# Seven-product pairs: product F in another PSUM bank, and sums, casts and low parts in another order

## The chip, the core and the metric

The kernel runs on one core of a Trainium2 chip. The metric is the time of one execution in microseconds on the device, as the median of timed runs. The engines are TensorE (PE in the profile; PEld is its weight load), VectorE (DVE), ScalarE (ACT), GpSimd (POOL) and SyncE (SP, which issues most transfers). Each works through its own queue in order, and engines wait for each other by semaphores.

## The reference

The reference is a two-layer block over 512 latent tokens of width 1024. What matters here is the MLP that ends each layer, and of it the one of the second layer:

```
def _sq_relu_mlp(h, w1, w2):
    return jnp.square(jax.nn.relu(h @ w1)) @ w2
...
h_lat = h_lat + mod_l[5] * _sq_relu_mlp(
    _modulate(_rmsnorm(h_lat, norm2_g[i]), mod_l[3], mod_l[4]), mlp_w1[i], mlp_w2[i])
```

`w1` is 1024 x 4096 and `w2` 4096 x 1024. All is float32 in and out.

## The kernel before

**High and low parts.** TensorE multiplies in `fp32r`. To keep precision, each operand is split: ScalarE casts it to a high part (line 163), and VectorE or POOL subtracts that from the source for the low part (line 164). A product is then three sets of matmuls: weights' high by activations' high, weights' high by activations' low, weights' low by activations' high.

**Blocks.** `mlp` runs four blocks of 1024 hidden columns. In a block a first phase makes the hidden tiles (f = 0 to 7: square of relu of `h @ w1`, as `gh` and `gl`), and a second phase multiplies them by `w2` (output tiles called `r`, eight weights). In the second layer, blocks 1 to 3 make their hidden tiles two at a time with `pair7`: four pairs in a block, 12 in all. Block 0 makes the activation sums that this needs (`act_sums`, the tiles `th`, split partly by POOL).

**A pair.** Two hidden tiles (2 x 128 columns) by 512 tokens are a 2 x 2 problem of blocks, and `pair7` forms it from seven products instead of eight. Each product is 12 matmuls of 128x256 (lines 1655, 1656, 1658). They are called A to G here, in the order in which TensorE has them:

| Product | Written to | Weights | 
|---|---|---|
| A, B | `px[:, x]`, `py[:, x]` | two halves of `w0` |
| C | `py[:, y]` | `w1`, first half |
| D | `pz[:, y]` | `w2`, first half |
| E | `px[:, y]` | `w3` |
| F | `px[:, x]` again | `w1`, second half |
| G | `pz[:, x]` | `w2`, second half |

`px`, `py` and `pz` are PSUM tiles of one bank each; `x` and `y` are their halves of 256 columns. A wait is set for a whole tile: TensorE may not write one half while an earlier reader of the other half has not finished.

VectorE joins the products: the sum `s1` of `py` and the copy `p1` of A (line 1715); `u3` from E (1721); two more sums into `s1` from D and F (1722, 1725); `s2` from G (1729). The `finish` function that a pair returns is called in the next pair: three ScalarE instructions for each of the two hidden tiles (relu, square to `gh`, square in place), and VectorE's low part `gl` for each (1741).

**Weights.** Of the four weights of a pair, `w0` is the raw weight k. `w1` is made from two sums by VectorE (`pair_sums`, lines 1430 and 1431), `w2` is the raw weight k + 1 after POOL has added its own halves (1439, the "second sum" here), and `w3` is a sum of two raw halves by POOL (1438, "early sum" here). VectorE makes the low parts of `w1` and `w2`, POOL those of `w0` and `w3`. `w_fetch` issues the transfers of raw weights on SP, `w_prep` makes the next weights ready. The order of each engine's queue is the order in which this code is written.

Of the kernel before, what the change touches and what calls it, by code (L numbers as in the profile page):

```python
# [12 lines left out]
ALU = mybir.AluOpType  # L13
# [8 lines left out]
T = 512  # L22
# [71 lines left out]
def body(ctx: ExitStack, tc: tile.TileContext, I, out):  # L94
    nc = tc.nc
    act = nc.scalar
    dve = nc.vector
    pool = nc.gpsimd
    pe = nc.tensor

    def f32(ap):
        return ap.bitcast(F32)
# [46 lines left out]
    def nm(s):  # L149
        cnt[0] += 1  # L150
        return f"{s}_{cnt[0]}"
# [10 lines left out]
    def split(hi, lo, src, lo_eng=None):  # L162
        act.copy(out=hi, in_=src)  # L163
        (lo_eng or dve).tensor_tensor(out=lo, in0=src, in1=f32(hi), op=ALU.subtract)  # L164
# [5 lines left out]
    def wfetch(src, which="s"):  # L170
        pl, tg, nr, nb, rp = streams[which]
        raw = rp.tile([P, 1024], F32, name=nm("raw"), tag=tg + "raw", bufs=nr)
        nc.sync.dma_start(out=raw, in_=src)
        return raw

    def wload(src, lo_eng, which="s", raw=None):
        pl, tg, nr, nb, rp = streams[which]
        if raw is None:
            raw = wfetch(src, which)
        hi = pl.tile([P, 1024], F32R, name=nm("whi"), tag=tg + "whi", bufs=nb)  # L180
        lo = pl.tile([P, 1024], F32R, name=nm("wlo"), tag=tg + "wlo", bufs=nb)
        split(hi, lo, raw, lo_eng)
        return hi, lo
# [22 lines left out]
    def proj(*a, late=0):  # L206
        for _ in proj_steps(*a, late=late):
            pass
# [93 lines left out]
    w3 = st.tile([P, 1024], F32, name="w3", tag="swhi", bufs=2)  # L302
# [56 lines left out]
    def row_load(k):  # L359
# [11 lines left out]
        out=sil, in0=e16.rearrange("p (s k) -> p s k", s=2), in1=prm[:, 0:16].rearrange("p (s k) -> p s k", s=2), op=ALU.mult  # L371
# [1004 lines left out]
    for d in range(3):  # L1376
        for k in (6, 7):
            out_part(8 * d + k)
        dve.scalar_tensor_tensor(
            out=hs[d], in0=r_pre[d], scalar=g1[:, d : d + 1], in1=hs[d], op0=ALU.mult, op1=ALU.add  # L1380
# [10 lines left out]
    def ps_m(name):  # L1391
        return ps.tile([P, T], F32, name=nm(name), tag="mm", bufs=6)
# [10 lines left out]
    wraw, wsp = [], []  # L1403
    fast = set(range(9)) | set(range(65, 77)) - {73}

    def w_fetch(n):
        while len(wraw) < min(n, len(wsrc)):
            k = len(wraw)
            wraw.append(ahead.pop(3 + k) if k < 3 else wfetch(wsrc[k], "st"[k % 2]))
# [2 lines left out]

    pairs, sums_done, scr = set(), set(), [None]

    def w_split(k, src, eng, n=1024):
        pl, tg, nr, nb, rp = streams["st"[k % 2]]
        hi = pl.tile([P, 1024], F32R, name=nm("whi"), tag=tg + "whi", bufs=nb)
        lo = pl.tile([P, 1024], F32R, name=nm("wlo"), tag=tg + "wlo", bufs=nb)  # L1420
        split(hi[:, :n], lo[:, :n], src, eng)
        return hi, lo

    def pair_sums(k):

        if k in sums_done or k not in pairs:
            return
        sums_done.add(k)
        a, b, t = wraw[k], wraw[k + 1], scr[0]
        dve.tensor_tensor(out=t[:, :T], in0=b[:, :T], in1=a[:, :T], op=ALU.add)  # L1430
        dve.tensor_tensor(out=t[:, T : 2 * T], in0=t[:, :T], in1=a[:, T:], op=ALU.add)

    def w_prep(n):
        while len(wsp) < min(n, len(wsrc)):
            k = len(wsp)
            if k in pairs:
                a, b, t = wraw[k], wraw[k + 1], scr[0]
                pool.tensor_tensor(out=t[:, 2 * T : 3 * T], in0=a[:, :T], in1=b[:, :T], op=ALU.add)
                pool.tensor_tensor(out=b[:, :T], in0=b[:, :T], in1=b[:, T:], op=ALU.add)
                wsp.append(w_split(k, a, pool))  # L1440
            elif k - 1 in pairs:
                pair_sums(k - 1)
                wsp.append(w_split(k, scr[0][:, : 2 * T], dve))
            else:
                eng = (dve, pool)[k // 2 % 2]
                wsp.append(wload(None, pool if k in fast else eng, "st"[k % 2], wraw[k]))
# [3 lines left out]
    def w_next(lead=2):  # L1450

        k = wk[0]
        wk[0] += 1
        w_fetch(k + 7)
        w_prep(k + 1 + lead)
        return wsp[k]
# [162 lines left out]
    def mlp(layer, ah_, al_, nrm, i_norm, shift_in, last_norm, mod_next, load=None, seven=True):  # L1619
# [25 lines left out]
        def b_part(half, t):  # L1645
            seg = slice(t * 256, (t + 1) * 256)
            return [(ah_[half * 4 + i][:, seg], al_[half * 4 + i][:, seg]) for i in range(4)]

        def t_part(n):
            return [(th[:, i, 0, n, :], th[:, i, 1, n, :]) for i in range(4)]  # L1650

        def product(o, w, c, b):
            for i in range(4):
                l = w[0][:, c + i * P : c + (i + 1) * P]
                pe.matmul(o, l, b[i][0], start=(i == 0), stop=False)  # L1655
                pe.matmul(o, l, b[i][1], start=False, stop=False)  # L1656
            for i in range(4):
                pe.matmul(o, w[1][:, c + i * P : c + (i + 1) * P], b[i][0], start=False, stop=(i == 3))  # L1658
        for blk in range(4):
# [35 lines left out]
            def pair7(f, before):  # L1695

                k = wk[0]
                wk[0] += 2
                w_fetch(k + 7)
                w0, w1 = wsp[k], wsp[k + 1]  # L1700
                w2 = w_split(k, wraw[k + 1], dve)
                x, y = slice(0, 256), slice(256, 512)
                px, py, pz = ps_m("f"), ps_m("f"), ps_m("f")
                small = [ml.tile([P, 256], F32, name=nm("na"), tag="na", bufs=4) for _ in range(2)]
                p1, u3 = small
                s1 = ml.tile([P, T], F32, name=nm("r"), tag="r", bufs=3)
                twice = lambda v: v.rearrange("p (a t) -> p a t", a=1).to_broadcast([P, 2, 256])
                both = lambda v: v.rearrange("p (a t) -> p a t", a=2)
                product(px[:, x], w0, 0, b_part(0, 0))
                act.copy(out=p1, in_=px[:, x])  # L1710
                product(py[:, x], w0, T, b_part(1, 0))
                w3 = w_split(k + 1, scr[0][:, 2 * T : 3 * T], pool, T)
                before(0)
                product(py[:, y], w1, 0, t_part(2))
                dve.tensor_tensor(out=both(s1), in0=both(py), in1=twice(p1), op=ALU.add)
                before(1)
                w_fetch(k + 9)
                w_prep(k + 3)
                product(pz[:, y], w2, 0, t_part(0))
                product(px[:, y], w3, 0, t_part(1))  # L1720
                dve.tensor_tensor(out=u3, in0=px[:, y], in1=s1[:, y], op=ALU.add)  # L1721
                dve.tensor_tensor(out=s1[:, y], in0=pz[:, y], in1=s1[:, y], op=ALU.add)
                pair_sums(k + 2)
                product(px[:, x], w1, T, b_part(1, 1))
                dve.tensor_tensor(out=s1[:, y], in0=px[:, x], in1=s1[:, y], op=ALU.add)
                w_prep(k + 4)
                product(pz[:, x], w2, T, [(ah_[i][:, y], al_[i][:, y]) for i in range(4)])
                s2 = ml.tile([P, T], F32, name=nm("r"), tag="r", bufs=3)
                dve.tensor_tensor(out=both(s2), in0=both(pz), in1=twice(u3), op=ALU.add)
                for u in range(2):  # L1730
                    mk = att_tile if f + u < 4 else w_tile
                    gh[f + u], gl[f + u] = mk("gh"), mk("gl")

                def finish(part):
                    for u, s, sign in ((0, s1, 1.0), (1, s2, -1.0)):
                        if part != 1:
                            act.activation(out=s, in_=s, func=AF.Relu, scale=sign)
                            act.activation(out=gh[f + u], in_=s, func=AF.Square)
                            act.activation(out=s, in_=s, func=AF.Square)
                        if part != 0:  # L1740
                            dve.tensor_tensor(out=gl[f + u], in0=s, in1=f32(gh[f + u]), op=ALU.subtract)

                return finish

            f0 = 0
            if blk == 0:
                f0 = 4
                n = 256
# [31 lines left out]
            if blk and seven:  # L1780
                fin7 = lambda part: None
                for f in range(0, 8, 2):
                    fin7 = pair7(f, fin7)
                fin7(2)
            else:
                for f in range(f0, 8):
                    w = w_next()
                    pp = f_tile(f)
                    proj(pp, w, ah_, al_)
                    f_out(f, 0, T, pp)  # L1790
                    if blk:
                        grow()
# [108 lines left out]
    for hf, (t0, n) in enumerate(SEG):  # L1901
        for d in range(ND):
# [4 lines left out]
            for k in range(3):  # L1907
                t = hf + k
                a, b = zh[t][d // 4][:, cs_], zl[t][d // 4][:, cs_]
# [225 lines left out]
```

## Time and profile before

| | us |
|---|---|
| Median of three runs | 1133.67 (1132.42 to 1134.82) |
| Profiled execution, its own time | 1134.61 |
| Its span (first to last instruction) | 1132.8 |
| PE busy | 1083.6 (96% of the span) |
| DVE busy | 769.3 (68%) |
| POOL busy | 492.3 (43%) |
| ACT busy | 480.3 (42%) |

The three blocks of pairs lie at about 844 to 897, 940 to 986 and 1030 to 1076 us of the span. The busy shares are means over the whole program; what an instruction waits for is read from the stretch in which it stands. A row's last bracket gives how long the engine had been idle before it and whose end it waited for.

### The profile page before, as it was taken

How to read it: one execution, taken by the hardware profiler on the slowest of the kernel's cores; microseconds unless marked ns; L12 is line 12 of the kernel's file. 1: busy time of each engine (PE TensorE's matmuls, PEld its weight loads, DVE VectorE, ACT ScalarE, POOL GpSimd, SP SyncE). 2: the span in 40 equal slices, each digit the busy share in tenths (PEclk: the TensorE clock that was granted, in tenths of full speed). 3: DMA queues.
4: the chain of work that ended last, by engine and by line, in shares of the span. 5: the costliest groups of instructions: out<-in, count | busy, mean ns of one | idle time of the engine just before them, and what ended most of it. 6: DMA issues, size and time to landing. Idle time of an engine off the chain costs nothing.

```text
span 1132.8 us, 15916 instructions
## 1 busy us (share of the span) xinstructions
PE 1083.6 (96%) x6172; PEld 934.0 (82%) x6172; DVE 769.3 (68%) x1114; ACT 480.3 (42%) x812; POOL 492.3 (43%) x364
## 2 busy tenths in 40 slices
PE   8899999999999999999999999899998899999896
PEld 5488988888989988888888888899878888889886
DVE  6589899989856746676686684776457626725844
ACT  4454246666544531341241232565325614713531
POOL 4457237785654322122122133363576525443512
PEclk9899999999999999999999999999999999999998
DMA  9776754125432336557567553122312322332212
GB/s 336 271 268 207 248 171 144 67 69 171 157 124 75 113 111 242 170 196 248 169 204 252 173 189 128 38 68 83 110 62 89 114 75 75 112 112 75 75 38 75
DMA packets 48654, 161.42 MB, mean 142 GB/s; under 512 B 5250, under 2 KB 8578, under 8 KB 48452
## 3 DMA queue, kind: packets, MB, share of 16 engines
q1 hardware_dynamic: 46132, 149.93, 38.6%
q0 software_dynamic: 2448, 10.49, 2.6%
q8 instruction: 48, 0.79, 0.3%
q14 instruction: 26, 0.21, 0.1%
HBM read 156.20 MB, written 4.20 MB: 142 GB/s over the span
## 4 chain that ended last, share of the span: by engine, by line
PE 71%; DVE 14%; ACT 4%; issue 4%; DMA 3%; POOL 3%; SPq 0%; POOLq 0%; ACTq 0%; DVEq 0%
PE r L197 11%; PE r L199 10%; PE r L203 10%; PE f L199 6%; PE f L203 6%; PE f L197 6%; DVE g L629 3%; PE f L1655 2%; PE f L1658 2%; PE f L1656 2%; DMA g<-in_adaN 1%; DMA g<-in_adaT 1%; DVE nl L1542 1%; DVE scr L1430 1%; ACT whi L163 1%
## 5 line engine op out<-in xcount | busy, mean ns | idle before, releaser
L164 POOL TENSOR_TENSOR wlo<-raw,whi 128x1024 fp32r<-128x1024 f32 x77 | 191.5, 2489 | 360.0 <-ACT whi L163 305.4
L197 PE MATMUL r<-gh,whi 128*128 128x512 f32 (+1 forms) x576 | 207.3, 368 | 0.0
L199 PE MATMUL r<-gl,whi 128*128 128x512 f32 (+1 forms) x576 | 207.0, 368 | 0.0
L163 ACT CAST whi<-raw 128x1024 fp32r<-128x1024 f32 x135 | 139.3, 1042 | 126.4 <-PE r L199 102.1
L1555 DVE SCALAR_TENSOR_TENSOR h<-r,mods,h 128x512 f32<-128x512 f32 (+1 forms) x81 | 54.3, 671 | 149.4 <-PE r L203 149.2
L203 PE MATMUL r<-gh,wlo 128*128 128x512 f32 (+1 forms) x576 | 130.7, 368 | 0.0
L197 PEld LDWEIGHTS r<-gh,whi 128*128 128x128 f32 x576 | 108.3, 188 | 19.1
L199 PEld LDWEIGHTS r<-gl,whi 128*128 128x128 f32 x576 | 108.4, 188 | 18.9
L203 PEld LDWEIGHTS r<-gh,wlo 128*128 128x128 f32 x576 | 100.5, 188 | 18.9
L197 PE MATMUL f<-nh,whi 128*128 128x512 f32 (+1 forms) x320 | 116.0, 370 | 0.0
L199 PE MATMUL f<-nl,whi 128*128 128x512 f32 (+1 forms) x320 | 116.0, 370 | 0.0
L1484 DVE CUSTOM_DVE_ANT_0 g<-g,sbcl 128x1024 f32<-128x1024 f32 x48 | 105.1, 2191 | 0.0
L1673 DVE TENSOR_TENSOR r<-r 128x512 f32<-128x512 f32 (+1 forms) x48 | 37.6, 784 | 67.9 <-ACT gh L1672 67.8
L164 DVE TENSOR_TENSOR wlo<-raw,whi 128x1024 fp32r<-128x1024 f32 x58 | 75.0, 1294 | 12.2 <-ACT whi L163 12.2
L1671 ACT ACTIVATE r<-f 128x512 f32<-128x512 f32 (+1 forms) x48 | 25.1, 523 | 131.6 <-PE f L203 130.0
L203 PE MATMUL f<-nh,wlo 128*128 128x512 f32 (+1 forms) x320 | 73.1, 371 | 0.0
L199 PEld LDWEIGHTS f<-nl,whi 128*128 128x128 f32 x320 | 60.2, 188 | 10.8
L197 PEld LDWEIGHTS f<-nh,whi 128*128 128x128 f32 x320 | 60.2, 188 | 10.8
L203 PEld LDWEIGHTS f<-nh,wlo 128*128 128x128 f32 x320 | 56.3, 188 | 10.8
L197 PE MATMUL u<-ah,whi 128*128 128x512 f32 x160 | 63.4, 396 | 1.3 <-DVE v L884 1.3
L199 PE MATMUL u<-al,whi 128*128 128x512 f32 x160 | 62.5, 391 | 0.0
L1655 PE MATMUL f<-nh,whi 128*128 128x256 f32 x192 | 48.9, 287 | 13.9 <-DVE na L1721 13.9
(413 smaller groups left out, 2514.9 us busy)
## 6 DMA issues: line engine op xcount, KB each, us to landing
raw<-in_w SPq DMA_DIRECT2D x128, 512.0 KB, 4.5
g<-in_adaT SPq DMA_DIRECT2D x80, 512.0 KB, 4.0
g<-in_adaN SPq DMA_DIRECT2D x16, 512.0 KB, 9.1
raw<-in_w_hy SPq DMA_DIRECT2D x12, 512.0 KB, 4.3
raw<-in_w_qk SPq DMA_DIRECT2D x8, 512.0 KB, 4.0
pth<-in_pth POOLq DMA_DIRECT2D x4, 768.0 KB, 5.9
raw<-in_w_out SPq DMA_DIRECT2D x5, 512.0 KB, 3.6
x<-in_xT SPq DMA_DIRECT2D x8, 256.0 KB, 7.1
```

The lines of the kernel that those rows point to most:

```text
L163: act.copy(out=hi, in_=src)
L164: (lo_eng or dve).tensor_tensor(out=lo, in0=src, in1=f32(hi), op=ALU.subtract)
L197: pe.matmul(ps, wh[:, c], ah[i][:, t0 : t0 + n], start=(i == 0), stop=False)
L199: pe.matmul(ps, wh[:, c], al[i][:, t0 : t0 + n], start=False, stop=False)
L203: pe.matmul(ps, wl[:, i * P : (i + 1) * P], ah[i][:, t0 : t0 + n], start=False, stop=(i == k - 1))
L629: dve.tensor_tensor_reduce(out=g, in0=g, in1=sbc[0], scale=1.0, scalar=0.0, op0=ALU.mult, op1=ALU.add, accum_out=mods[:, 0, 2 + k // ND, k ...
L1484: dve.tensor_tensor_reduce(out=gin[k], in0=gin[k], in1=sbc[0], scale=1.0, scalar=0.0, op0=ALU.mult, op1=ALU.add, accum_out=mods[:, layer, ...
L1555: dve.scalar_tensor_tensor(out=hs[d][:, seg], in0=pp[:, :n], scalar=gate[:, d : d + 1], in1=hs[d][:, seg], op0=ALU.mult, op1=ALU.add)
L1655: pe.matmul(o, l, b[i][0], start=(i == 0), stop=False)
L1656: pe.matmul(o, l, b[i][1], start=False, stop=False)
L1671: act.activation(out=r, in_=pp[:, :n], func=AF.Relu)
L1673: dve.tensor_tensor(out=r, in0=r, in1=r, op=ALU.mult)
```

## The change

The change works in `pair7` and its helpers alone.

- F is written to `py[:, x]` instead of `px[:, x]`, and the sum behind it reads it there.
- POOL's two sums for the next pair get a function of their own, `pair_first`. It is called early in a pair, the first of the two sums ahead of the split of `w3`, the second behind it; for this the sum has two places in `scr` that take turns (`s3_part`).
- The split of `w3` (cast and low part) is moved from behind B to ahead of A.
- The weight sums of the next pair (`pair_sums`) are moved from behind VectorE's sums on D and E to ahead of them.
- `finish` now runs in four calls: ScalarE's three instructions of the first hidden tile, its low part, then (behind the cast of the next `w0`) ScalarE's three of the second, and its low part only after VectorE's sums on D and E.
- One fetch at the start of a pair, up to weight k + 7, takes the place of two, up to k + 6 and later k + 8.

```
-                w_fetch(k + 7)
+                w_fetch(k + 8)
+                pair_first(k + 2, 1)
                 w0, w1 = wsp[k], wsp[k + 1]
                 w2 = w_split(k, wraw[k + 1], dve)
+                w3 = w_split(k + 1, s3_part(k), pool, T)
+                pair_first(k + 2)
...
                 product(py[:, x], w0, T, b_part(1, 0))
-                w3 = w_split(k + 1, scr[0][:, 2 * T : 3 * T], pool, T)
                 before(0)
                 product(py[:, y], w1, 0, t_part(2))
                 dve.tensor_tensor(out=both(s1), in0=both(py), in1=twice(p1), op=ALU.add)
                 before(1)
-                w_fetch(k + 9)
                 w_prep(k + 3)
+                before(4)
+                pair_sums(k + 2)
                 product(pz[:, y], w2, 0, t_part(0))
                 product(px[:, y], w3, 0, t_part(1))
                 dve.tensor_tensor(out=u3, in0=px[:, y], in1=s1[:, y], op=ALU.add)
                 dve.tensor_tensor(out=s1[:, y], in0=pz[:, y], in1=s1[:, y], op=ALU.add)
-                pair_sums(k + 2)
-                product(px[:, x], w1, T, b_part(1, 1))
-                dve.tensor_tensor(out=s1[:, y], in0=px[:, x], in1=s1[:, y], op=ALU.add)
+                before(2)
+                product(py[:, x], w1, T, b_part(1, 1))
+                dve.tensor_tensor(out=s1[:, y], in0=py[:, x], in1=s1[:, y], op=ALU.add)
                 w_prep(k + 4)
...
-                        if part != 1:
+                        if part in (4 * u, 3):
...
-                        if part != 0:
+                        if part in (u + 1, 3):
```

```
+    def s3_part(k):
+        c = (2 + k // 2 % 2) * T
+        return scr[0][:, c : c + T]
+
+    def pair_first(k, n=2):
+
+        if k not in pairs:
+            return
+        a, b = wraw[k], wraw[k + 1]
+        if (k, 1) not in first_done:
+            first_done.add((k, 1))
+            pool.tensor_tensor(out=s3_part(k), in0=a[:, :T], in1=b[:, :T], op=ALU.add)
+        if n == 2 and (k, 2) not in first_done:
+            first_done.add((k, 2))
+            pool.tensor_tensor(out=b[:, :T], in0=b[:, :T], in1=b[:, T:], op=ALU.add)
```

Lines move by the added code: 1715, 1721, 1722, 1725, 1729 and 1741 become 1731, 1738, 1739, 1742, 1746 and 1758; 1438 and 1439 become 1444 and 1447.

VectorE's queue in the second pair of the first block, before. The tiles `f` are PSUM, `r` is `s1` or `s2`, `na` is `u3` or `p1`, `scr` and `raw` hold weights:

```order
L1715 TENSOR_TENSOR r_8092<-f_8088,na_8090 128x512
L1741 TENSOR_TENSOR gl_8080<-r_7967,gh_8079 128x512
L1741 TENSOR_TENSOR gl_8082<-r_8077,gh_8081 128x512
L1721 TENSOR_TENSOR na_8091<-f_8087,r_8092 128x256
L1722 TENSOR_TENSOR r_8092<-f_8089,r_8092 128x256
L1430 TENSOR_TENSOR scr_7169<-raw_7914,raw_7873 128x512
L1431 TENSOR_TENSOR scr_7169<-scr_7169,raw_7873 128x512
L1725 TENSOR_TENSOR r_8092<-f_8087,r_8092 128x256
```

The same place on VectorE after:

```order
L1731 TENSOR_TENSOR r_8100<-f_8096,na_8098 128x512
L1758 TENSOR_TENSOR gl_8078<-r_7975,gh_8077 128x512
L1430 TENSOR_TENSOR scr_7169<-raw_7914,raw_7873 128x512
L1431 TENSOR_TENSOR scr_7169<-scr_7169,raw_7873 128x512
L1738 TENSOR_TENSOR na_8099<-f_8095,r_8100 128x256
L1739 TENSOR_TENSOR r_8100<-f_8097,r_8100 128x256
L1758 TENSOR_TENSOR gl_8080<-r_8075,gh_8079 128x512
L1742 TENSOR_TENSOR r_8100<-f_8096,r_8100 128x256
```

The two weight sums stand ahead of `u3` and of the sum behind it now, one of the two low parts behind them; and the last row reads the tile of the first (`f_8096`, `py`) instead of that of `u3`.

POOL's queue from the same pair on, before (`wlo<-scr` is the low part of `w3`, `wlo<-raw` that of the next `w0`):

```order
L164 TENSOR_TENSOR wlo_8119<-scr_7169,whi_8118 128x512
L1438 TENSOR_TENSOR scr_7169<-raw_7873,raw_7914 128x512
L1439 TENSOR_TENSOR raw_7914<-raw_7914 128x512
L164 TENSOR_TENSOR wlo_8150<-raw_7873,whi_8149 128x1024
L164 TENSOR_TENSOR wlo_8252<-scr_7169,whi_8251 128x512
L1438 TENSOR_TENSOR scr_7169<-raw_7956,raw_8010 128x512
```

The same place on POOL after:

```order
L1444 TENSOR_TENSOR scr_7169<-raw_7873,raw_7914 128x512
L164 TENSOR_TENSOR wlo_8091<-scr_7169,whi_8090 128x512
L1447 TENSOR_TENSOR raw_7914<-raw_7914 128x512
L164 TENSOR_TENSOR wlo_8144<-raw_7873,whi_8143 128x1024
L1444 TENSOR_TENSOR scr_7169<-raw_7956,raw_7958 128x512
L164 TENSOR_TENSOR wlo_8224<-scr_7169,whi_8223 128x512
```

The early sum of the next pair stands ahead of the low part of `w3`, and so directly behind the 1024-wide low part of `w0` of the pair before.

## Rows read from the trace of the kernel before

**Rows 1.** Whom TensorE waited for: engine, line, releaser, us in total, times, longest.

```profile
PE f L1655 <- DVE na L1721: 13.9, 12, 1.6
```

**Rows 2.** Timeline of TensorE, first block: start us, length us, instruction, [idle before, releaser].

```profile
868.84 0.39 PE L1655 MATMUL f<-nh,whi 128*128 128x256 f32 x1 [1.59 <-DVE na L1721]
...
870.37 0.28 PE L1655 MATMUL f<-nh,whi 128*128 128x256 f32 x1
...
871.79 0.28 PE L1655 MATMUL f<-nh,whi 128*128 128x256 f32 x1
...
881.14 0.38 PE L1655 MATMUL f<-nh,whi 128*128 128x256 f32 x1 [1.59 <-DVE na L1721]
...
893.22 0.39 PE L1655 MATMUL f<-nh,whi 128*128 128x256 f32 x1 [1.37 <-DVE na L1721]
```

**Rows 3.** Timeline of VectorE, same stretch.

```profile
867.54 0.91 DVE L1741 TENSOR_TENSOR gl<-r,gh 128x512 fp32r<-128x512 f32 x1 [0.78 <-ACT r L1739]
868.37 0.41 DVE L1721 TENSOR_TENSOR na<-f,r 128x256 f32<-128x256 f32 x1
868.82 0.43 DVE L1722 TENSOR_TENSOR r<-f,r 128x256 f32<-128x256 f32 x1
869.62 2.86 DVE L1430 TENSOR_TENSOR scr<-raw,raw 128x512 f32<-128x512 f32 x1 [0.38 <-POOL raw L1439]
...
876.14 1.22 DVE L164 TENSOR_TENSOR wlo<-raw,whi 128x1024 fp32r<-128x1024 f32 x1
```

**Rows 4.** Timeline of POOL, same stretch.

```profile
869.55 2.38 POOL L164 TENSOR_TENSOR wlo<-raw,whi 128x1024 fp32r<-128x1024 f32 x1
```

**Rows 5.** Chain of waits, one turn of the ring: start us, length us, piece.

```profile
876.19 2.34 POOL wlo L164
...
880.28 1.62 POOL raw L1439
...
881.92 2.86 DVE scr L1430
...
884.81 0.70 DVE scr L1431
```

**Rows 6.** Timeline of ScalarE: first of six squares, and the cast behind them.

```profile
876.00 0.63 ACT L1737 ACTIVATE r<-r 128x512 f32<-128x512 f32 x1
...
879.71 1.03 ACT L163 CAST whi<-raw 128x1024 fp32r<-128x1024 f32 x1
```

**Rows 7.** Timeline of the second block: A, `p1`, `s1` of its first pair; F of its fourth.

```profile
940.37 0.28 PE L1655 MATMUL f<-nh,whi 128*128 128x256 f32 x1
...
941.98 0.38 ACT L1710 COPY na<-f 128x256 f32<-128x256 f32 x1 [2.68 <-PE f L1658]
...
944.87 0.69 DVE L1715 TENSOR_TENSOR r<-f,na 128x512 f32<-128x512 f32 x1 [2.42 <-PE f L1658]
...
983.12 0.39 PE L1655 MATMUL f<-nh,whi 128*128 128x256 f32 x1 [1.37 <-DVE na L1721]
```

**Rows 8.** Timeline of the first pair of the first block, several engines.

```profile
844.93 0.68 DVE L1430 TENSOR_TENSOR scr<-raw,raw 128x512 f32<-128x512 f32 x1
...
850.71 0.39 PE L1655 MATMUL f<-th,whi 128*128 128x256 f32 x1 [2.18 <-ACT th L163]
...
851.42 0.73 POOL L164 TENSOR_TENSOR nl<-b,nh 128x256 fp32r<-128x256 f32 x1
...
852.17 1.22 DVE L164 TENSOR_TENSOR wlo<-raw,whi 128x1024 fp32r<-128x1024 f32 x1 [1.55 <-ACT whi L163]
...
857.06 0.39 PE L1655 MATMUL f<-nh,whi 128*128 128x256 f32 x1 [0.52 <-DVE na L1721]
```

**Rows 9.** Stretches: us, busy (instructions) of PE, PEld, DVE, ACT, POOL; granted clock, DMA share, GB/s.

```profile
851.50:854.90 3.40, 3.39 (x17) 3.39 (x18) 1.83 (x2) 2.38 (x4) 2.46 (x3) 0.55 0.01 2
...
870.40:873.80 3.40, 3.40 (x31) 3.40 (x30) 3.10 (x3) 0.49 (x1) 1.53 (x1) 1.00 0.02 5
```

**Rows 10.** DMA issues on the page: transfer, queue, count, KB each, us to landing.

```profile
raw<-in_w SPq DMA_DIRECT2D x128, 512.0 KB, 4.5
```

More of the change, by code (lines that the diff above doesn't have):

```diff
@@ L1409, in w_fetch @@
             wraw.append(ahead.pop(3 + k) if k < 3 else wfetch(wsrc[k], "st"[k % 2]))
-    pairs, sums_done, scr = set(), set(), [None]
+    pairs, first_done, sums_done, scr = set(), set(), set(), [None]
     def w_split(k, src, eng, n=1024):
@@ L1436, in w_prep @@
             if k in pairs:
[L1437 to L1440, printed above, removed]
+                pair_first(k)
+                wsp.append(w_split(k, wraw[k], pool))
             elif k - 1 in pairs:
@@ L1783, in mlp @@
                     fin7 = pair7(f, fin7)
-                fin7(2)
+                fin7(3)
             else:
```

## Prediction

> **What bounds the kernel now.** I read first the page's busy shares (TensorE 96%), then whom TensorE waits for, then the stretch where it waits, engine by engine. The longest sum of waits is one group: the first matmul of product F waits for VectorE's `u3` (line 1721), 13.9 us in 12 times, once in each of the 12 pairs [rows 1]. Everything the change touches lies in these 12 pairs, so the rest of the 1132.8 us span is taken over as it is.
>
> In a pair without waits TensorE needs seven products. One is 1.42 us (871.79 less 870.37), so seven are 9.95 us; the pair from F to F lasts 12.30 us (881.14 less 868.84) [rows 2]. It is tempting to book the whole 1.59 us wait before F as a gain. But the rows of the other engines show why `u3` is late. VectorE reaches `u3` at 868.37, having waited for ScalarE before the second low part `gl` at 867.54 [rows 3]; and the chain of waits in this stretch runs not through TensorE but in a ring: POOL's low part (876.19) and second weight sum (880.28), VectorE's weight sums 1430 and 1431 (881.92, 884.81), then ScalarE's casts and squares, and round again [rows 5].
>
> The price inside this ring is that VectorE and POOL hold each other up. VectorE's sum 1430 lasts 2.86 us at 869.62 beside POOL's low part of 869.55 to 871.93, and ends 0.55 us after it [rows 3, 4]; with POOL idle the same sum is 0.68 us [rows 8]. The other way round, POOL's 512-wide low part (876.19, 2.34 us) ends 1.17 us after VectorE's low part of 876.14 to 877.36 [rows 3, 5]. VectorE's sums that read PSUM don't pay: `u3` takes 0.41 us at 868.37 while POOL works towards 869.55. So in these rows POOL's work and VectorE's work with two SBUF operands take turns, in the order in which they ask. The Trainium skill (SBUF — State Buffer, "Who interferes with whom") calls the shared pair an exclusive lock, held for a whole instruction; these rows agree, and the rule speaks against putting such a VectorE instruction between two that TensorE waits for. If POOL cost VectorE nothing, the stall below would be nil and the time that of the second rival.
>
> **The change, part by part.** Times in this part count from the first matmul of a pair's product A.
>
> *The banks.* F goes to `py[:, x]` instead of `px[:, x]`. It then waits not for `u3`, which reads E's result, but for the sum `s1`, which reads `py` at 4.50 us (944.87 less 940.37 [rows 7]); F's natural start is 5 x 1.42 = 7.1 us. That wait goes, all 13.9 us of it. What is late next is G: it writes `pz`, which the second half of `s1` (line 1739 after) reads, directly behind `u3` in VectorE's queue. G's natural start is 6 x 1.42 = 8.53 us.
>
> *VectorE's queue.* Before, `u3` stood behind two low parts. Now the queue is sum `s1`, low part of the pair before (`gl`, u = 0), the two weight sums 1430 and 1431 of the next pair, and only then `u3` and line 1739. The weight sums are moved ahead of what TensorE waits for. Take the second pair of a block. The copy `p1` starts at 1.61 us and takes 0.38 [rows 7]; three of ScalarE's six squares then last half of 3.71 us (876.00 to 879.71) [rows 6], so the cast for the next `w0`, moved up by three squares, runs from 3.85 to about 4.9 us (1.03 [rows 6]), and POOL's low part of it (2.38 us [rows 4]) from 4.95 to 7.35. VectorE's sum ends at 5.2 [rows 7]; `gl` asks at 5.1, gets its turn at 7.35 and ends at 7.9. POOL's next instruction is the early sum for the pair after next (it was moved ahead of POOL's low part for `w3`); it asks at 7.35, waits for `gl`, and takes a turn of 1.15 us [rows 5] to 9.05. Sum 1430 ends 0.55 us after that, 9.6; sum 1431 adds 0.7 [rows 5]: 10.3; `u3` 0.42 and line 1739 0.45 more [rows 3]: 11.2. G starts 2.7 us late. If `gl` asked just before POOL, the order of the turns would differ and the end hardly.
>
> In the third pair no early sum follows (there is no pair after next): `gl` 7.9, 1430 at 8.5, 1431 at 9.2, line 1739 at 10.1, so G is 1.6 us late. In the fourth there are no weight sums: 8.75, 0.25 us late. In the first there is no `gl` to write, but 1430 meets POOL's low part and 1431 the early sum: 0.1 us if POOL's low part follows its cast at once, 0.8 if POOL was first held up by `w2`'s low part; I take 0.5. Each restart costs 0.1 more (after the wait F takes 1.53 instead of 1.42 us, 870.37 less 868.84 [rows 2]).
>
> *Sum for the second and third block.* From A of the first pair to G of the fourth: 3 x 9.95 + 8.53 + 5.05 of waits + 0.3 of restarts = 43.75 us. Before: 983.12 + 1.53 - 940.37 = 44.28 [rows 7]. That is -0.5 us each, -1.0 together: the stall is moved from F to G.
>
> *Sum for the first block.* Here POOL comes late out of the activation sums: its last low part ends at 852.15, and VectorE's `w2` low part starts at 852.17 [rows 8]. The order after is early sum, low part of `w3`, second sum, low part of `w0`: early sum until 854.5 (behind `w2`, 1.22 us), then two of at least 1.17 us to 856.9, then 2.4 to 859.3. Weight sum 1430 needs that second sum and then meets the low part of `w0`: 859.9; another early sum 861.0; 1431 at 861.6, line 1739 at 862.5. Before, F started at 857.06 after 0.52 us of waiting [rows 8], so G at 858.6; now G comes at about 862.6: +4.0 us. The three pairs behind it then take 3 x 9.95 + 4.55 + 0.3 = 34.7 us from G to G, against 36.16 before (893.22 less 857.06 [rows 2, 8]): -1.5. The block costs +2.5 us.
>
> *Nothing from:* the fetches. They bring the same tiles in the same order on SP, two pairs ahead of use; a raw weight lands 4.5 us after its issue [rows 10], and two pairs are some 20 us; if that cover were gone, an early sum would hold POOL up for as long as 4.5 us. Products, casts and sums are as many as before.
>
> *The clock.* After the wait of 2.18 us at 850.71 [rows 8] the granted clock of the next 3.4 us is 0.55 of full, near the 1.2 GHz level, and 17 matmuls start in it; after the 1.59 us wait before F it stays at 1.00, and 31 start [rows 9]. A lost stretch so costs up to 14 x 0.118 (1.42 / 12) = 1.65 us. The new waits of 2.7 us (three) and of over 4 us (one) are longer than the one that lost it. From nothing to all four: 0 to 6.6 us. I take two of four at two thirds of the price, since part of the slow stretch lies where G would wait anyhow: +2.1. [...]
>
> *In all:* -1.0 + 2.5 + 2.1 = +3.6 us. The profiled execution took 1134.61 us, 0.94 above the median of the three timed runs; on the median the forecast is 1133.67 + 3.6 = **1137.3 us**.
>
> **The rivals.** (1) The wait moves from F to G as above, but no stretch loses the clock, and the first block loses less: 0 to +2 us, 1133.7 to 1135.8. For it: three waits of 1.6 us cost no clock. Against: 2.18 us did. (2) Faster: VectorE meets POOL once, not twice. If the early sum gets its turn only after the weight sums, the second pair goes as the third, 1.1 us less in each block, and the first block's POOL work hides behind its slow start: about -4 us, 1129.5. If VectorE met POOL nowhere, line 1739 would end at 7.9, before 8.53, and 13.9 us of waits with their restarts would go: about 1118. The point from which it decides is 0.55 us: the early sum asks at 7.35, sum 1430 at 7.9, and only if POOL's were the later of the two would it hold. For it: the turns are settled within tenths of a microsecond. Against: POOL's next instruction stands ready in its queue, as the second sum did at 880.28. (3) All four long waits lose the clock in full: 1.5 + 6.6 = +8.1, 1141.8. That F would still wait (the change not doing what it says) needs `s1` to be 2.6 us late; nothing stands before it but one low part.
>
> **How the numbers follow.** Forecast (over 1135.9, up to 1141.5): 0.52. Rival 1: 0.26. Rival 2: 0.16. Rival 3 and beyond 1141.5: 0.06. The range reaches from rival 2's first figure to just short of rival 3: 1130 to 1141.5, leaving out about 2 in 10. About 0.2% (2.3 us) is what a measurement of this kernel can tell from no change; so faster 0.16, the same 0.26, slower 0.58.
>
> **What would show it.** In the profile after: TensorE's waits for line 1738 gone; a new group, the matmul of G waiting for line 1739, some 13 to 16 us in 9 to 12 times, with two long ones per block, the longest in the first pair of the first block; line 1430 still 1.5 to 1.8 us in most pairs and the first `gl` of a pair near 2.8 us; granted clock below 1 behind some of the long waits. Wrong if G's waits sum to under 10 us, if `gl` is short, or if the fetches show in POOL's waits.

## The result, and the profile of the kernel after

| | Before | After |
|---|---|---|
| Median of five runs each, us | 1134.15 (1132.42 to 1135.69) | 1139.29 (1138.61 to 1143.24) |
| Ratio | | 1.0056, interval 1.0033 to 1.008 |
| Profiled execution, us | 1134.61 | 1138.79 |

The change makes the kernel slower by about half a per cent. From one profiled execution to the other it is 4.2 us, on the medians 5.1; the forecast was 3.6.

The page of the kernel after begins so; TensorE's work is the same, and it is spread over a longer span:

```profile
span 1137.0 us, 15915 instructions
PE 1084.9 (95%) x6172; PEld 937.1 (82%) x6172; DVE 772.9 (68%) x1114; ACT 482.4 (42%) x812; POOL 490.4 (43%) x364
```

The first thing to look up is the group that stood at the head of TensorE's waits, [rows 1]. In the waits of after (us in total, times, longest) no wait for `u3` (line 1738 now) is left, and this stands in its place:

```profile
PE f L1669 <- DVE r L1739: 16.2, 9, 3.9
```

So F doesn't wait any more, and G waits for the sum behind `u3`, in nine of the twelve pairs. The timeline of TensorE shows the single waits (start us, length us, instruction, [idle before, releaser]); these are G of the first to fourth pair of the first block, of the first three of the second, and of the second and third of the third block:

```profile
862.98 0.58 PE L1669 MATMUL f<-nh,whi 128*128 128x256 f32 x1 [3.93 <-DVE r L1739]
...
876.92 0.39 PE L1669 MATMUL f<-nh,whi 128*128 128x256 f32 x1 [2.41 <-DVE r L1739]
...
888.45 0.39 PE L1669 MATMUL f<-nh,whi 128*128 128x256 f32 x1 [1.33 <-DVE r L1739]
...
898.65 0.39 PE L1669 MATMUL f<-nh,whi 128*128 128x256 f32 x1
...
953.65 0.39 PE L1669 MATMUL f<-nh,whi 128*128 128x256 f32 x1 [0.64 <-DVE r L1739]
...
966.29 0.39 PE L1669 MATMUL f<-nh,whi 128*128 128x256 f32 x1 [2.44 <-DVE r L1739]
...
977.82 0.39 PE L1669 MATMUL f<-nh,whi 128*128 128x256 f32 x1 [1.35 <-DVE r L1739]
...
1055.66 0.39 PE L1669 MATMUL f<-nh,whi 128*128 128x256 f32 x1 [2.43 <-DVE r L1739]
...
1068.39 0.39 PE L1669 MATMUL f<-nh,whi 128*128 128x256 f32 x1 [1.02 <-DVE r L1739]
```

Why line 1739 is late stands in VectorE's timeline of the second pair of the first block, where before `u3` came at 868.37 [rows 3]:

```profile
870.35 0.69 DVE L1731 TENSOR_TENSOR r<-f,na 128x512 f32<-128x512 f32 x1 [2.58 <-PE f L1672]
870.96 2.70 DVE L1758 TENSOR_TENSOR gl<-r,gh 128x512 fp32r<-128x512 f32 x1
873.58 1.77 DVE L1430 TENSOR_TENSOR scr<-raw,raw 128x512 f32<-128x512 f32 x1
875.38 0.69 DVE L1431 TENSOR_TENSOR scr<-scr,raw 128x512 f32<-128x512 f32 x1
875.99 0.42 DVE L1738 TENSOR_TENSOR na<-f,r 128x256 f32<-128x256 f32 x1
876.45 0.42 DVE L1739 TENSOR_TENSOR r<-f,r 128x256 f32<-128x256 f32 x1
```

and beside it in that of POOL:

```profile
870.71 2.40 POOL L164 TENSOR_TENSOR wlo<-raw,whi 128x1024 fp32r<-128x1024 f32 x1 [0.53 <-ACT whi L163]
873.06 1.74 POOL L1444 TENSOR_TENSOR scr<-raw,raw 128x512 f32<-128x512 f32 x1
```

`gl` (0.68 us with POOL idle, as the second one at 876.78) lasts until 0.55 us after POOL's low part has ended (873.66 against 873.11); POOL's early sum ends 1.14 us after `gl` (874.80); sum 1430 ends 0.55 us after that (875.35). POOL's low part, `gl`, the early sum and sum 1430 take turns. `u3` and line 1739, 0.42 us each, are not held up by POOL themselves; they stand behind all of that in VectorE's queue. No wait for a transfer stands among the waits of the engines in the pairs, so the fetches play no part, as the prediction had it.

### The profile page after: what moved, and what is told of

The parts are those of the page before. It is cut to its first block, busy times and chain, and to the rows that moved or that the text cites. A ratio compares the mean times of both kernels' runs of the same rounds, so it can differ in the third digit from the quotient of the medians.

```text
span 1137.0 us, 15915 instructions
## 1 busy us (share of the span) xinstructions
PE 1084.9 (95%) x6172; PEld 937.1 (82%) x6172; DVE 772.9 (68%) x1114; ACT 482.4 (42%) x812; POOL 490.4 (43%) x364
## 4 chain that ended last, share of the span: by engine, by line
PE 71%; DVE 16%; issue 3%; ACT 3%; POOL 3%; DMA 3%; SPq 0%; POOLq 0%; DVEq 0%; ACTq 0%
PE r L197 11%; PE r L199 10%; PE r L203 10%; PE f L199 6%; PE f L203 6%; PE f L197 6%; PE f L1669 2%; DVE g L629 2%; PE f L1672 2%; PE f L1670 2%; DVE gl L1758 1%; PE v L878 1%; DVE nl L1556 1%; DVE scr L1430 1%; DMA g<-in_adaN 1%
## 5 line engine op out<-in xcount | busy, mean ns | idle before, releaser
L1669 PE MATMUL f<-nh,whi 128*128 128x256 f32 x192 | 50.8, 296 | 16.2 <-DVE r L1739 16.2
```

## Where the 4.2 us lie

The three blocks can be measured from A of the first pair to the first matmul of the second phase. In TensorE's timeline of after:

```profile
845.40 0.28 PE L1669 MATMUL f<-nh,whi 128*128 128x256 f32 x1
...
900.17 0.39 PE L197 MATMUL r<-gh,whi 128*128 128x512 f32 x1
...
944.36 0.28 PE L1669 MATMUL f<-nh,whi 128*128 128x256 f32 x1
...
989.56 0.39 PE L197 MATMUL r<-gh,whi 128*128 128x512 f32 x1
...
1033.74 0.28 PE L1669 MATMUL f<-nh,whi 128*128 128x256 f32 x1
...
1080.12 0.39 PE L197 MATMUL r<-gh,whi 128*128 128x512 f32 x1
```

Of before the same six are at 844.67, 896.18, 940.37, 986.07, 1030.26 and 1075.97.

| | Before, us | After, us | Difference | Forecast without the clock |
|---|---|---|---|---|
| Block 1 | 51.51 | 54.77 | +3.26 | +2.5 |
| Block 2 | 45.70 | 45.20 | -0.50 | -0.5 |
| Block 3 | 45.71 | 46.38 | +0.67 | -0.5 |

With the 0.73 us by which the first of these matmuls already comes later, and 0.05 us behind the last, that is the difference of the spans. No term of the forecast covers the 0.73 us: this matmul comes anywhere from 844.07 to 848.62 us in the profiles of this case. Blocks 2 and 3 have the same instructions, and they differ by 1.18 us although block 3 waits 0.33 us less before its third G. The windows say why (us, busy time and instructions of PE, PEld, DVE, ACT and POOL; then the granted clock, the DMA share, GB/s):

```profile
862.40:865.80 3.40, 2.82 (x13) 2.82 (x14) 2.05 (x4) 1.55 (x2) 0.00 (x0) 0.53 0.73 248
1057.00:1060.40 3.40, 3.40 (x18) 3.40 (x18) 2.40 (x3) 1.92 (x4) 1.80 (x1) 0.52 0.65 265
966.30:969.70 3.40, 3.40 (x29) 3.40 (x29) 3.40 (x5) 2.14 (x5) 0.47 (x1) 1.00 0.75 298
877.00:880.40 3.40, 3.40 (x29) 3.40 (x30) 3.40 (x5) 2.13 (x5) 0.53 (x1) 1.00 0.85 308
```

Behind the waits of 3.93 and of 2.43 us the granted clock is 0.53 and 0.52, near the level of 1.2 GHz; behind those of 2.41 and 2.44 us it stays at 1.00. So in this execution two of the four long waits lost a stretch of clock. In block 3 the stretch slows TensorE by 1.18 + 0.33 = 1.5 us, beside the 1.65 at which the prediction had bounded it; 0.33 of that lies where the third G would have waited anyhow, so 1.2 us are left to pay.

## The experiments

The theory: line 1739 is late because VectorE's instructions with two SBUF operands (`gl`, 1430, 1431) meet POOL and stand ahead of it; the bank by itself gains little; and waits of over 2 us cost clock on top. The rivals: the bank decides; POOL's new order, not VectorE's, holds up G; or VectorE has simply too much work there.

### The bank alone

The kernel before, with F in `py`:

```
-                product(px[:, x], w1, T, b_part(1, 1))
-                dve.tensor_tensor(out=s1[:, y], in0=px[:, x], ...
+                product(py[:, x], w1, T, b_part(1, 1))
+                dve.tensor_tensor(out=s1[:, y], in0=py[:, x], ...
```

> The kernel before with one edit: F is written to and read from the py tile; the order of every queue stays. Theory of the ring (the pairs are paced by POOL, VectorE and ScalarE in turn, and the wait before F only shows it): the wait moves to G and to low parts of weights; most of the 13.9 us stays, time 2 to 5 us below before, 1129 to 1132. Rival, the bank was the whole cause: all 13.9 us and the restarts go, 1118 to 1121.

1131.28 us, 0.9971 of before [0.9954, 0.9987]. The 13.9 us of [rows 1] are gone, and 3.5 us are gained. Among TensorE's waits:

```profile
PE f L1655 <- DVE r L1722: 3.7, 7, 0.6
```

G now waits, for the sum behind `u3`, which reads `pz`; and sum 1430, as in [rows 3], is still 2.87 us long (at 873.37). The rest shows itself in the waits of TensorE's weight loads, from 840 to 1085 us:

```profile
PEld f L1655 <- DVE r L1722: 5.7, 9, 0.8
...
PEld f L1658 <- DVE wlo L164: 3.8, 15, 0.3
...
PEld f L1655 <- ACT whi L163: 3.4, 7, 0.5
...
PEld f L1658 <- POOL wlo L164: 2.1, 7, 0.5
```

That is 15.0 us, where the loads of before waited 17.5 (16.3 for `u3`, 1.2 for low parts). So the wait is not gone, it has spread over G and the high and low parts of the weights. A wait that heads the list can be the place where a ring shows itself, not its cause: who takes the wait away is left with the ring.

### The order alone

The kernel after, with F back in `px`, so that only the order is changed against before.

> The changed kernel with F back in the px tile; the new order of the queues stays. Theory: F now waits for u3, which stands behind the weight sums, 1 us longer than G did: waits of 30 us and more, some over 3 us long, and lost clock behind them; time 1147 to 1157. Rival, the bank does nothing either way: 1139.

1157.89 us, 1.021 [1.0185, 1.0234].

```profile
PE f L1669 <- DVE na L1738: 26.6, 12, 3.5
```

The waits came out somewhat shorter than expected, the time a little above. The waits of F grow by 12.7 us over [rows 1] and the time by 23; the rest is clock at least in part, by the windows from 840 to 910 us of this kernel and of after (before had 0.98 there):

```profile
840.00:910.00 70.00, 56.68 (x366) 53.81 (x365) 45.02 (x49) 30.29 (x45) 34.89 (x21) 0.83 0.21 76
```

```profile
840.00:910.00 70.00, 59.73 (x404) 55.45 (x403) 47.96 (x53) 35.79 (x52) 39.16 (x23) 0.95 0.26 91
```

So the change is a gain and a larger loss: the order costs 2.1%, and with that order the bank gives 1.5% back, since it lets G wait, one product later, instead of F.

### The weight sums back behind line 1739

```
                 before(4)
-                pair_sums(k + 2)
...
                 before(2)
+                pair_sums(k + 2)
```

> The changed kernel with the two weight sums (1430, 1431) put back behind u3 and the sum behind it. Theory (the weight sums ahead of what TensorE waits for are what made G late): G's waits fall from 16.2 us to under 5, the granted clock is lost nowhere but behind the wait at 850, time 1124 to 1128, that is 11 to 15 us below the changed kernel. Rival, POOL's early sum or the split low parts are the cause: still over 1134.

1127.81 us, 0.9938 [0.9919, 0.9957], as expected. G waits no more for line 1739. What TensorE waits for instead is a low part that VectorE makes:

```profile
PE f L1672 <- DVE wlo L164: 6.4, 8, 1.0
```

All eight stand behind the low part of `w2`, made from a raw weight, as here in the second block:

```profile
965.08 2.16 DVE L164 TENSOR_TENSOR wlo<-raw,whi 128x1024 fp32r<-128x1024 f32 x1
967.29 0.74 PE L1672 MATMUL f<-th,wlo 128*128 128x256 f32 x4 [0.99 <-DVE wlo L164]
```

It too has two SBUF operands: it takes 2.16 us beside POOL's low part of `w3` here, and 1.21 in the last pair of the block, where POOL doesn't work at that time.

### The first low part behind line 1739

```
-                before(1)
                 w_prep(k + 3)
...
+                before(1)
                 before(2)
```

> The changed kernel with only the first low part gl moved behind u3 and line 1739; the weight sums stay ahead. Theory: the sums still meet POOL's low part of w0 and then the early sum, so G's longest waits fall by some 0.6 us only: 1132 to 1136. If gl rather than the weight sums is what holds G up: 1125 or less.

1132.34 us, 0.9985 [0.9969, 1.0001]; G still waits, 12.4 us in all. VectorE's timeline shows that the sum 1430 has simply taken over the turn of `gl`:

```profile
869.84 2.67 DVE L1430 TENSOR_TENSOR scr<-raw,raw 128x512 f32<-128x512 f32 x1
872.54 1.66 DVE L1431 TENSOR_TENSOR scr<-scr,raw 128x512 f32<-128x512 f32 x1
```

It is not one instruction that is too many; whichever stands first behind the sum `s1` meets POOL's low part, and the next meets the early sum.

### Both behind line 1739

```
-                before(1)
                 w_prep(k + 3)
                 before(4)
-                pair_sums(k + 2)
...
+                pair_sums(k + 2)
+                before(1)
                 before(2)
```

> The changed kernel with the weight sums and both low parts of the pair before behind u3 and line 1739, so that VectorE's queue has no instruction with two SBUF operands between the first sum of a pair and what TensorE waits for. Theory: no wait over 1 us is left in the pairs of blocks 2 and 3, one in block 1; time 1118 to 1122, 12 to 16 us below before. Rival, POOL and VectorE are simply too full in a pair of 9.95 us (they hold each other up for as long wherever the sums stand) and weights come late instead: 1130 or more.

1118.76 us, 0.9866 [0.9845, 0.9886]: 16 us under before, so it beats both kernels. There is no wait for the sum behind `u3`. In VectorE's timeline of the second pair it now comes straight behind the product, and the sums behind it find POOL nearly done with its low part (867.21 to 869.60):

```profile
868.78 0.42 DVE L1737 TENSOR_TENSOR r<-f,r 128x256 f32<-128x256 f32 x1
869.12 1.03 DVE L1430 TENSOR_TENSOR scr<-raw,raw 128x512 f32<-128x512 f32 x1
870.18 1.67 DVE L1431 TENSOR_TENSOR scr<-scr,raw 128x512 f32<-128x512 f32 x1
```

Sum 1431 still meets the early sum, but nothing that TensorE needs stands behind. Line 1430 as a group (times, shortest/median/longest ns, first and last start), first of this kernel and then of after:

```profile
L1430 DVE TENSOR_TENSOR scr<-raw,raw x12: 680/684/1850, 844.5 to 1048.9; 128x512 f32<-128x512 f32 x12
```

```profile
L1430 DVE TENSOR_TENSOR scr<-raw,raw x12: 678/1160/2848, 845.7 to 1066.1; 128x512 f32<-128x512 f32 x12
```

And TensorE is busy for 44.68 of the 45 us from 940 to 985, which hold most of the second block and the start of its second phase, at full clock, where before waited 1.2 us in each pair (13.9 in 12):

```profile
940.00:985.00 45.00, 44.68 (x342) 42.86 (x341) 32.13 (x43) 29.43 (x43) 23.86 (x13) 1.00 0.30 107
```

### That order with the old bank

The kernel of the section before, with F back in `px`.

> The order of e4_all_behind (weight sums and low parts behind u3 and line 1739), but F back in the px tile, so that F waits for u3 again. Theory: u3 then comes straight after E, so F waits 0.6 to 0.8 us in each of the 12 pairs, 8 us in all, no more; time 7 us above e4_all_behind, 1125 to 1128, still below before. Rival, with the order mended the bank is worth nothing: 1119.

1126.21 us, 0.9942 [0.9921, 0.9963]. F waits for `u3` again, but briefly:

```profile
PE f L1669 <- DVE na L1736: 6.2, 12, 0.5
```

So the bank is worth 0.3% with the order of before, 1.5% with that of the change, and 0.8% once VectorE's order is right. It is a good change in each of the three; only the order that came with it is bad.

### No meeting with POOL

If VectorE had just too much to do ahead of line 1739, the same instructions in the same order would be slow without POOL in their way. Here one operand of `gl` and of both weight sums is a PSUM tile of zeros; the count and shape of the instructions stay.

```
+        c = other_[0] if other_ else a[:, :T]
-        dve.tensor_tensor(out=t[:, :T], in0=b[:, :T], in1=a[:, :T], op=ALU.add)
+        dve.tensor_tensor(out=t[:, :T], in0=b[:, :T], in1=c, op=ALU.add)
...
-  dve.tensor_tensor(out=gl[f + u], in0=s, in1=f32(gh[f + u]), ...
+  dve.tensor_tensor(out=gl[f + u], in0=s, in1=other_[0], ...
```

> The changed kernel, each queue in its order, but one SBUF operand of the low parts gl and of the weight sums 1430 and 1431 is replaced by a PSUM tile of zeros (these values are then not the reference's). Theory (these instructions are long only because they take turns with POOL): gl and 1430 take 0.7 us each time, G waits for nothing, time 1115 to 1119. Rival, the queue order alone makes G late, whatever the length: waits stay over 10 us, 1133 or more.

1117.05 us, 0.986 [0.9836, 0.9884]. Line 1430 (1433 here) takes 0.68 us each time, from the first pair on whose tile of zeros exists, and of G's wait one of 0.7 us is left:

```profile
L1433 DVE TENSOR_TENSOR scr<-raw,oth x11: 676/679/687, 856.4 to 1043.6; 128x512 f32<-128x512 f32 x11
```

```profile
PE f L1672 <- DVE r L1742: 0.7, 1, 0.7
```

That settles it: with the order of the change unaltered, taking the second SBUF operand away is worth 23.8 us, the lost clock included, against the kernel after on the same chip (1140.86, below). The sums also stop reading one of the raw weights, but VectorE waits for no transfer in the pairs of either kernel, so that is not where the time went. The Trainium skill (SBUF — State Buffer, "Who interferes with whom") says that a VectorE instruction with two SBUF inputs contends with a POOL instruction that reads SBUF, and calls the ports that they share an exclusive lock. The pair of kernels agrees: the median of the sum is 1.16 us with two SBUF operands and 0.68 with one.

### The place of POOL's early sum

The kernel after, with the early sum behind the low part of `w3` as before:

```
                 w_fetch(k + 8)
-                pair_first(k + 2, 1)
```

> The changed kernel with POOL's early sum put back behind the low part of w3, as before the change; all else as changed. Theory: both POOL sums then stand between the low part of w3 and that of w0, the low part of w0 and with it the first low part gl come later; G's waits grow to 20 us or more, time 1140 to 1146. Rival, the early sum ahead of w3 is what makes G late: 1134 or less.

1141.81 us, 1.0075 [1.0054, 1.0095]; G's wait is 18.0 us where 20 or more were expected:

```profile
PE f L1669 <- DVE r L1738: 18.0, 9, 3.4
```

The kernel after took 1139.79 beside it (1.0054 [1.0035, 1.0073]), so the two intervals lie over each other. The early sum's new place is no cause of the loss; that it helps by up to 2 us is not shown. The split of `w3` and the fetches stayed as changed in this run, and no run moved them alone.

> The changed kernel beside the two above, for a comparison on one chip: 1138 to 1143.

That run is the one just named; its wait of G is 16.1 us in 9 times, against 16.2 of the first.

### The clock

If the waits of G cost clock on top, matmuls that fill them should give back that part and leave the wait. The kernel after, with matmuls into an unused PSUM tile just ahead of the four long G, 26 in the first pair of the first block and 16 in the second pair of each block:

```
+   idle_fill = {(1, 0): 26, (1, 2): 16, (2, 2): 16, (3, 2): 16}.get((blk, f), 0)
+   if idle_fill:
+       fill = ps.tile([P, T], F32, name=nm("fill"), tag="tr", bufs=2)
+       for _ in range(idle_fill):
+           pe.matmul(fill[:, :256], w2[0][:, T : T + P], ah_[0][:, y], start=True, stop=True)
                 product(pz[:, x], w2, T, ...
```

(`f` counts hidden tiles, so `f` = 2 is the second pair.)

> The changed kernel with extra matmuls into a spare PSUM tile just before G, where G waits longest: 26 in the first pair of the first block, 16 in the second pair of each block (they change no result; 0.118 us each, so 3.1 and 1.9 us of work inside waits of 3.9 and 2.4 us). Theory (2.1 us of the 3.6 forecast is clock lost behind long waits): no stretch behind these waits at the lower clock, less scatter, 1135 to 1137, 2 to 5 us below the changed kernel. Rival, the clock is lost by chance and not by these waits: 1139, or longer by the added matmuls.

> The changed kernel once more, beside the three above: 1138 to 1143, G's waits 16 us, two to four stretches of lost clock behind them.

1135.6 us with the filling, 1.0007 [0.9992, 1.0022]; 1140.86 without on the same chip, 1.0062 [1.004, 1.0084]. The work added is useless, and the kernel is 5.3 us faster for it. The windows of the filled kernel, where after had 0.53 and 0.52:

```profile
862.40:865.80 3.40, 2.45 (x21) 2.25 (x20) 3.15 (x6) 1.96 (x2) 0.00 (x0) 1.00 0.55 157
1057.00:1060.40 3.40, 3.40 (x31) 3.40 (x31) 1.69 (x2) 3.06 (x7) 2.51 (x2) 1.00 0.42 172
```

31 matmuls start in the second of them, 18 in that of after. In TensorE's timeline of the filled kernel the three blocks, measured as above, run from 845.95 to 899.45, from 943.66 to 988.83 and from 1033.04 to 1078.18 us: 53.50, 45.17 and 45.14 us, 0.9 us more than before in all. The profile of after has 2.5 us more than that, for two lost stretches.

The two other profiles of after lost more. That on this chip (1143.53 us) shows G's four long waits as 1.99 us at 866.22, 2.43 at 880.35, 2.44 at 971.24 and 2.42 at 1061.89, and behind them:

```profile
866.40:869.80 3.40, 3.40 (x19) 3.40 (x20) 2.49 (x4) 1.69 (x3) 0.23 (x1) 0.56 0.87 306
880.20:883.60 3.40, 3.25 (x15) 3.25 (x16) 2.49 (x5) 1.60 (x3) 0.00 (x0) 0.53 0.82 282
971.80:975.20 3.40, 3.40 (x21) 3.40 (x20) 3.18 (x4) 1.57 (x2) 1.02 (x1) 0.62 0.79 301
1062.00:1065.40 3.40, 3.40 (x29) 3.40 (x30) 3.40 (x5) 2.15 (x5) 0.57 (x1) 1.00 0.84 301
```

Three of four waits lost the clock, and so they did in the third profile of after, at 1142.80 us. The blocks of these two add up to 4.3 us more than those of the filled kernel. So a lost stretch cost between 1.2 and 1.5 us here, and the size of the wait alone doesn't say whether the clock falls: 1.99 us lost it, 2.42 us kept it, and 2.44 us lost it here and kept it in the first profile.

## Why the prediction was right, and which term was mis-sized

**Where the wait goes.** As forecast: 1738 gone, G waiting for 1739, 16.2 us in 9 times, the longest in the first pair of the first block; the second and third blocks have two of over a microsecond each, 2.4 and 1.0 to 1.35.

**VectorE's queue.** Counted from the end of the sum `s1` in the second pair (5.2 in the prediction, 871.04 in the trace), `gl`, 1430, 1431 and 1739 should end after 2.7, 4.4, 5.1 and 6.0 us; they end after 2.62, 4.31, 5.03 and 5.83. The waits are 2.4 instead of 2.7, 1.3 instead of 1.6, 0.64 instead of 0.5, and none instead of 0.25. The rule of turns, taken from two rows of before, carried this part of the forecast. Rival 2's condition (the early sum asks after sum 1430) did not arise: POOL's early sum begins at 873.06, sum 1430 at 873.58, and POOL has the first turn. Its other half, VectorE meeting POOL nowhere, was put at 1118; the experiment with the PSUM operand gives 1117.05.

**One sign that failed.** Line 1430 was to take 1.5 to 1.8 us in most pairs. Five of its twelve instructions take 1.64 to 1.77, one 2.85, and six 0.68. The prediction's own queue had it short in the third pairs, where no early sum follows.

**The second and third block.** -0.5 was forecast, -0.50 is the second block. The third is +0.67; without its lost stretch it would be about -0.6 (45.14 in the filled kernel).

**The first block.** G of the first pair was forecast at 862.6, 17.9 us after A; it comes at 862.98, 17.6 after A. The three pairs behind it take 35.67 us (898.65 less 862.98) for 34.7: the shorter waits take off 0.8, the lost stretch adds 1.3 (from the first G to the second 13.94 us, in the filled kernel 12.63), and 0.5 stay unexplained. Without the stretch the block is 2.0 us longer than before (53.50), not 2.5.

**The clock: the term that was mis-sized.** The forecast was 2.1 us: two of four waits, each at two thirds of 1.65 (which makes 2.2). The first profile had indeed two, at 1.2 to 1.3 us each. But the two later ones had three, and there a stretch cost up to 1.5. Filling the waits gave back 5.3 us of the median, and without them the kernel stands at 1.0007, inside the 0 to +2 us of rival 1 and a little under the -1.0 + 2.5 of the other terms. That is why the median differences, 5.1, 6.1 and 6.9 us in three comparisons, all lie above the 3.6. That some waits would lose the clock and some not was right; the count was too low for the median, and the price of one stretch somewhat too low.

**Where luck came in.** That the first profile lies so near the forecast (3.4 us in the blocks for 3.6) is in part luck: the first block without the clock was put 0.5 us too high, and the clock of that execution 0.4 too low. With three lost stretches, as in the two other profiles, the blocks are 5.2 us longer than before.

**What stays open.** Why one wait of 2.4 us loses the clock and the next does not; and why single executions of before scatter from 1131 to 1139 us. Part of such scatter lies ahead of the pairs: where the first A came latest (848.62), the granted clock from 362 to 374 and from 724 to 736 us was 0.72, in the profile of before 0.86.

## What to carry to other kernels

An instruction queue is a list of who delays whom: put what TensorE waits for ahead of anything that another engine can hold up, and the same instructions cost some 21 us less here (1.0056 against 0.9866). Before believing that a wait at the head of the list is worth its sum, follow it one step further: taken away alone, 13.9 us of waits gave 3.5, because the ring behind them stayed. And price a long wait twice, once for its length and once for the clock behind it.

## What was not expected of the hardware

That the clock's price varies so much from one execution to the next of the same kernel: two of the four long waits lost a stretch in the profile at 1138.79 us, three in those at 1143.53 and 1142.80. The Trainium skill (TensorE: Matmul & The Clock Gate, "What's actually happening") has the clock fall when the engine has been idle for a while. The three profiles agree in that each fall in the pairs stands behind a wait, but the waits of 2.41, 2.42 and 2.44 us that kept 1.00, beside those of 1.99, 2.43 and 2.44 us that did not, show that a wait's length doesn't tell which it will be. Matmuls whose result nobody reads were enough to keep the clock.
